# A hybrid decoder trunk on one core: the feed-forward input by Strassen's scheme on 6144 of 11264 columns, with the tokens stationary

## The chip, the core and the metric

One core of one Trainium2 chip runs the whole program in one launch. The metric is the device time of an execution in microseconds; of the kernel before three runs were timed. Engine names are those of the profile: PE is TensorE (PEld its weight loads), DVE VectorE, ACT ScalarE, POOL GpSimd, SP the engine that issues the DMAs.

## The reference

Two layers on 256 tokens of width 2048, all in float32. Layer 0 is a recurrent block (RG-LRU), layer 1 windowed attention with sinks; each is followed by the same feed-forward block, with hidden width 5632:

```
def swiglu_ffn(x, g, w_in, w_out):
    h = rms_norm(x, g)
    gate, up = jnp.split(h @ w_in, 2, axis=-1)
    return x + (jax.nn.silu(gate) * up) @ w_out
```

`w_in` is 2048 x 11264 (5632 gate and 5632 up columns). The change is about the product `h @ w_in`, which occurs twice.

## The kernel before, in words

**Weights as a stream of jobs.** All weights are cut into tiles of 128x1024 float32 (512 KB): two blocks of 128 input rows by four blocks of 128 columns. `stream` (line 272) goes through the list of jobs, one tile each. It issues a tile's DMA four jobs ahead (`LD`), into one of four buffers `raw`, and splits the tile three jobs ahead (`LC`): `split` (line 255) makes the rounded high part `hi` on ACT (line 260) and the rest `lo = raw - hi` on DVE (line 261). `hi` and `lo` have four buffers each.

**Matmuls.** Activations lie transposed (features on the partitions, 256 tokens along the row) and are split in the same way into 256 high and 256 low columns of one slot `s`. A job computes, for 2 x 4 blocks, `hi*xhi + hi*xlo + lo*xhi`: 24 matmuls with the weights stationary and 256 moving columns (line 324), or, where two belong together, one with 512. A group of eight jobs gives four blocks of 128 output columns in four PSUM banks. In the feed-forward input such a group holds two hidden tiles, gate and up of each; 22 groups give all 44.

**Beside the stream.** Other work is written as generators that `run_bg` (line 201) steps through, some at every half job, as long as a budget of DVE and ACT time per half job (`DVE_TICK`, `ACT_TICK`) lasts. `need` forces them on when a matmul wants a value that is not there yet. In `ffn` (line 513) the finished group is pulled out of PSUM, multiplied with the norm's factor `rstd`, put through Silu, multiplied and split for the output projection (`split_act`, line 411). The norm's factor is applied after the product, so that the product doesn't wait for the norm. The helpers `a`, `tt`, `stt`, `ts` record one ACT or DVE instruction each and carry their line (114, 123, 127, 132, 134) in the profile; `pe_other` (line 328) records PE's side work.

**POOL** runs only in the attention (lines 925, 927, 969). In `kv` (line 745) the shared key is spread over both partition halves by four matmuls with selection matrices `K_SEL0` and `K_SEL1` (line 796). The recording layer puts each engine's instructions into one list, which the engine goes through in order.

Of the kernel before, what the change touches and what calls it, by code (L numbers as in the profile page):

```python
# [17 lines left out]
P = 128  # L18
D = 2048
T = 256  # L20
# [15 lines left out]
K_ONE, K_BLK, K_SEL0, K_SEL1, K_ID = 0, 128, 256, 384, 512  # L36
K_HS, K_MASK = 640, 672
K_PREV, K_OWN = 672 + 384, 672 + 512
NCON = 672 + 640
# [10 lines left out]
class Trunk:  # L50
# [14 lines left out]
    RUNS = 3  # L65
    DVE_TICK = 640.0
# [188 lines left out]
    def split(self, i):  # L255
        raw, hi, lo = self.raw[i % 4], self.hi[i % 4], self.lo[i % 4]
# [15 lines left out]
    def stream(self):  # L272
        n = len(self.jobs)
        self.warm()
        for i in range(-self.LD, n):
            self.tick = 2 * i
            if i + self.LD < n:
                self.load(i + self.LD)
            if 0 <= i + self.LC < n:
                self.split(i + self.LC)  # L280
            if i >= 0:
                self.jobs[i][1](self.hi[i % 4], self.lo[i % 4])
            else:
                self.half_tick()
            self.run_bg()
        self.drain()

# [53 lines left out]
    def group(self, src, nk, xs, done, last=False, sync=(), paired=False, jobs=None, packed=False):  # L341
# [6 lines left out]
        for c in range(nk // 2):  # L348
            def mm(hi, lo, c=c):
                if c == 0:  # L350
# [13 lines left out]
                    st["begun"] = set()  # L364
                    self.hold = False
# [88 lines left out]
    def norm(self, r, wait=NORM):  # L454
# [8 lines left out]
        for b in range(2):  # L463
            self.pe_other(ps[:, T + b:T + b + 1], self.acc[:, b * P:(b + 1) * P],
                          self.con[:, K_ONE:K_ONE + 1], start=True, stop=True)
        yield 1
        y = self.rstd[r]
        m, t = self.nm, self.nt
        self.ts(m, ps[:, 0:T + 2], 1.0 / D, EPS, ALU.mult, ALU.add)
# [43 lines left out]
    def ffn(self, l, xs, r, gains, rn, out=None):  # L513
        hid = [Val() for _ in range(NH)]
        w = self.d[f"ffn_in{l}"]
        for g in range(NH // 2):
            def done(ps, g=g):
                rs = self.rstd[r][:, 0:T]
                early = not self.rv[r].ready
                v = [self.pull(p, r=None if early else rs) for p in ps]  # L520

                def task():
                    while not self.rv[r].ready:
                        yield 1
                    for h in range(2):
                        ga, up = v[2 * h], v[2 * h + 1]
# [5 lines left out]
                        self.tt(ga, ga, up, ALU.mult)  # L532
                        while not self.slots:
                            yield 1
                        s = self.slot()
# [209 lines left out]
    def kv(self, xs, r, gains):  # L745
# [7 lines left out]
        def done(ps):  # L753
# [5 lines left out]
            def task():  # L759
# [39 lines left out]
                for h in range(4):  # L799
                    self.split_act(self.kd[h].ap, ps[h // 2][:, h % 2 * T:h % 2 * T + T])  # L800
                    if h % 2:
                        self.free_mbank(ps[h // 2])
# [340 lines left out]
```

## Time and profile before

| | |
|---|---|
| median of 3 runs | 1984.31 us (1984.11 to 1984.93) |
| the profiled execution's own time | 1983.45 us |
| its span, first to last instruction | 1981.7 us |
| mean granted clock of TensorE | 1.0 |
| busy in the span: PE, DVE, ACT, POOL | 1975.0, 1257.6, 1063.0, 71.1 us |
| HBM read | 372.01 MB, 189 GB/s over the span |

The span lies inside the execution's time; 1.75 us are around it. A row of the profile's groups gives the line, the engine, the operation, what it writes and reads by the program's names, the shape, the count, then busy us and the mean in ns of one, then the idle time of the engine just before them and what ended it. A row of the timeline gives start, length, engine, line and operation; with x2 it stands for two in a row. Matmuls are pipelined, so a mean of PE is longer than the distance from one start to the next.

### The profile page before, as it was taken

How to read it: one execution, taken by the hardware profiler on the slowest of the kernel's cores; microseconds unless marked ns; L12 is line 12 of the kernel's file. 1: busy time of each engine (PE TensorE's matmuls, PEld its weight loads, DVE VectorE, ACT ScalarE, POOL GpSimd, SP SyncE). 2: the span in 40 equal slices, each digit the busy share in tenths (PEclk: the TensorE clock that was granted, in tenths of full speed). 3: DMA queues.
4: the chain of work that ended last, by engine and by line, in shares of the span. 5: the costliest groups of instructions: out<-in, count | busy, mean ns of one | idle time of the engine just before them, and what ended most of it. 6: DMA issues, size and time to landing. Idle time of an engine off the chain costs nothing.

```text
span 1981.7 us, 40161 instructions
## 1 busy us (share of the span) xinstructions
PE 1975.0 (100%) x16691; PEld 1932.8 (98%) x16691; DVE 1257.6 (63%) x1981; ACT 1063.0 (54%) x1608; POOL 71.1 (4%) x100
## 2 busy tenths in 40 slices
PE   9999999999999999999999999999999999999999
PEld 9999999999999999999999889999999999999999
DVE  8988876556556655545667776755665565554443
ACT  7798755444444444434556775644544454444342
POOL 0000000000000000000001451000000000000000
PEclk9999999999999999999999999999999999999999
DMA  8555655665566556566655345566666666666664
GB/s 283 189 183 182 213 192 192 195 197 192 192 193 195 195 194 192 193 194 197 193 184 168 129 128 163 189 194 197 194 192 194 193 190 199 193 193 205 206 207 127
DMA packets 105302, 376.71 MB, mean 190 GB/s; under 512 B 11808, under 2 KB 14240, under 8 KB 105120
## 3 DMA queue, kind: packets, MB, share of 16 engines
q1 hardware_dynamic: 104832, 374.01, 58.9%
q8 instruction: 130, 2.13, 0.4%
q14 instruction: 52, 0.43, 0.1%
q10 hardware_dynamic: 288, 0.14, 0.0%
HBM read 372.01 MB, written 2.10 MB: 189 GB/s over the span
## 4 chain that ended last, share of the span: by engine, by line
PE 96%; DVE 2%; ACT 2%; issue 0%; DMA 0%; POOL 0%; SPq 0%; ACTq 0%
PE b L324 92%; PE b L646 1%; ACT s L114 1%; PE b L335 1%; DVE s L905 1%; PE b L837 1%; ACT hi L260 0%; DVE lo L261 0%; PE b L332 0%; DMA raw<-in_lru_in 0%; DVE s L123 0%; PE b L847 0%; PE b L846 0%; PE b L848 0%; PE b L322 0%
## 5 line engine op out<-in xcount | busy, mean ns | idle before, releaser
L324 PE MATMUL b<-s,hi 128*128 128x256 f32 (+1 forms) x10317 | 1432.2, 284 | 1.2 <-ACT s L114 0.6
L324 PEld LDWEIGHTS b<-s,hi 128*128 128x128 f32 x10317 | 1316.1, 188 | 31.5 <-issue 1.4
L261 DVE TENSOR_TENSOR lo<-raw,hi 128x1024 fp32r<-128x1024 f32 (+1 forms) x705 | 861.7, 1223 | 654.0 <-ACT hi L260 652.1
L260 ACT ACTIVATE hi<-raw 128x1024 fp32r<-128x1024 f32 (+1 forms) x705 | 745.7, 1059 | 813.8 <-PE b L324 757.9
L324 PE MATMUL b<-s,lo 128*128 128x256 f32 x5504 | 827.8, 276 | 0.0
L324 PEld LDWEIGHTS b<-s,lo 128*128 128x128 f32 x5504 | 718.1, 188 | 0.5
L925 POOL TENSOR_TENSOR s<-s 128x128 f32<-128x128 f32 x32 | 14.6, 458 | 1109.6 <-ACT s L114 1100.9
L114 ACT ACTIVATE s<-h 128x256 fp32r<-128x256 f32 (+1 forms) x106 | 40.7, 411 | 23.9 <-DVE h L123 23.9
L114 ACT ACTIVATE t<-b 128x256 f32<-128x256 f32 x132 | 48.6, 374 | 2.2
L114 ACT ACTIVATE s<-x,par 128x256 fp32r<-128x256 f32 x80 | 38.5, 499 | 19.4 <-DVE x L123 13.7
L114 ACT ACTIVATE s<-s 128x256 f32<-128x256 f32 (+1 forms) x112 | 40.0, 412 | 5.7 <-DVE s L127 5.5
L114 ACT ACTIVATE h<-h 128x256 f32<-128x256 f32 (+1 forms) x104 | 38.9, 376 | 4.8 <-DVE h L123 2.7
L114 ACT ACT_TABLE_LOAD x30 | 38.5, 1283 | 0.5
L127 DVE SCALAR_TENSOR_TENSOR s<-x,par,s 128x256 fp32r<-128x256 f32 x80 | 37.2, 479 | 1.3 <-ACT s L114 0.7
L114 ACT ACTIVATE s<-s,h 128x128 f32<-128x128 f32 x64 | 28.3, 442 | 17.8 <-DVE h L132 10.8
L123 DVE TENSOR_TENSOR x<-x,b 128x256 f32<-128x256 f32 x64 | 24.1, 416 | 21.2 <-PE b L324 21.2
L123 DVE TENSOR_TENSOR h<-b,rstd 128x256 f32<-128x256 f32 x100 | 37.5, 414 | 0.0
L123 DVE TENSOR_TENSOR h<-h,rstd 128x256 f32<-128x256 f32 x94 | 35.3, 417 | 0.0
L123 DVE TENSOR_TENSOR h<-h,h 128x256 f32<-128x256 f32 x88 | 34.7, 416 | 0.4 <-ACT h L114 0.4
L123 DVE TENSOR_TENSOR s<-h,s 128x256 fp32r<-128x256 f32 x88 | 34.9, 417 | 0.1
L123 DVE TENSOR_TENSOR s<-s,s 128x256 fp32r<-128x256 f32 (+1 forms) x80 | 31.2, 419 | 5.7 <-ACT s L114 5.6
L123 DVE TENSOR_TENSOR h<-b,t 128x256 f32<-128x256 f32 x92 | 34.5, 415 | 0.0
(99 smaller groups left out, 625.4 us busy)
## 6 DMA issues: line engine op xcount, KB each, us to landing
raw<-in_ffn_in SPq DMA_DIRECT2D x352, 512.0 KB, 3.8
raw<-in_ffn_out SPq DMA_DIRECT2D x176, 512.0 KB, 4.2
raw<-in_lru_in SPq DMA_DIRECT2D x63, 512.0 KB, 4.0
raw<-in_lru_out SPq DMA_DIRECT2D x32, 512.0 KB, 4.3
raw<-in_w_q SPq DMA_DIRECT2D x32, 512.0 KB, 3.5
raw<-in_w_o SPq DMA_DIRECT2D x32, 512.0 KB, 3.5
raw<-in_gate SPq DMA_DIRECT2D x8, 512.0 KB, 4.3
raw<-in_kv SPq DMA_DIRECT2D x8, 512.0 KB, 4.4
```

Source lines behind the costliest of these rows:

```text
L114: self.nc.scalar.activation(out, in_, func, **kw)
L123: self.nc.vector.tensor_tensor(out, a, b, op)
L127: self.nc.vector.scalar_tensor_tensor(out, a, s, b, op0, op1)
L260: self.nc.scalar.activation(hi[:, q], raw[:, q], AF.Copy)
L261: self.nc.vector.tensor_tensor(lo[:, q], raw[:, q], hi[:, q].bitcast(F32), ALU.subtract)
L324: self.nc.tensor.matmul(*args, **kw)
L335: self.other = self.ins(f(*args, **kw))
L646: nc.tensor.matmul(out[j], (hi if high else lo)[:, c:c + P], x2[kt][:, q:q + T], start=kt == 0 and high > q, stop=kt == 1 and not high)
L837: nc.tensor.matmul(ps[f][:, 0:T], w0, x2[kt][:, q:q + T], start=k0 + kt == 0 and high > q, stop=k0 + kt == ND - 1 and not high)
L905: nc.vector.tensor_tensor_reduce(sc[hh][:, c0:c1], ps[hh][:, c0:c1], con[:, K_MASK + c0:K_MASK + c1], rr[:, b * 8 + f * 2 + hh:b * 8 + f * ...
L925: nc.gpsimd.tensor_tensor(o, o, sc[hh][:, 2 * P:3 * P], ALU.add)
```

## The change

The feed-forward input gets a plan of its own. Of 44 hidden tiles, six are computed as before (three head groups, kind W, while the norm is not known yet), then come six units, then one last group W. A unit is 16 steps in the order of `UNIT`: eight of kind S and eight of kind C.

- **S** takes four hidden tiles: 512 gate and 512 up columns. Tokens (2 x 128), input rows (2 x 1024) and columns (gate, up) are halved, and for each pair of row blocks p and p+8 the four weight blocks b11, b12, b21, b22 (128x512 each) and four token blocks give seven products in place of eight. The tokens are stationary, the 512 weight columns move; each product is three matmuls (high and low parts). Its two weight tiles are two jobs, of which the first carries two products and the second five. The seven weight operands are b11, b22, b21 and the differences t1 = b12 - b11, t2 = b22 - t1, t3 = b22 - b12, t4 = t2 - b21. DVE makes t1 and t2, POOL t3 and t4. Each of the seven is split: `hi` on ACT, `lo` on DVE for five and on POOL for two (b11 and t3).
- **C** is an ordinary weight tile: four row blocks by gate and up of one hidden tile, 24 matmuls of 256 columns into one bank.
- The seven products accumulate over the eight S steps of a unit in seven banks, C has the eighth. `four` adds them up at the unit's end (one ACT copy, seven DVE instructions of 512 columns), makes Silu and product, and eight PE transposes with ACT copies bring the result back to features on the partitions.
- `hi` and `lo` are now a ring of eight half tiles of 512 columns; a split goes ahead while the ring and three jobs allow.
- Normalised tokens (`nrm`) and their four sums and differences per pair (`mix`) are prepared and split once the norm is known; the sums are 4 x 8 POOL instructions of 128x128 a layer. Finished hidden tiles are kept unsplit and are split for the output projection behind the last unit (`activations`).
- Elsewhere: the key's spread in `kv` is four DMAs on ACT's queue (64 partitions x 512) in place of the four matmuls, the two narrow matmuls of a norm are left out where their result isn't used (three of four norms), and in the attention the mark that holds the side work back ends a job later.

Core of the diff:

```
+    UNITS, HEAD = 6, 3
+    UNIT = "SSCSCCSCSSCSCCSC"
+    SPARSE = (60.0, 120.0)
...
+        def ahead(i):
+            nonlocal split
+            while split < len(items):
+                j, at, size, f, _ = items[split]
+                if j > i + self.LC or at + size - 8 > freed:
+                    break
+                if f is None:
+                    self.split(j, at // 2 % 4)
+                else:
+                    f(j, *self.block(at))
+                split += 1
...
+            while done < len(items) and items[done][0] == i:
+                _, at, size, f, mm = items[done]
+                assert split > done
+                done += 1
+                if f is None:
+                    mm(self.hi[at // 2 % 4], self.lo[at // 2 % 4])
+                    freed = at + size
+                else:
+                    mm(*self.block(at))
+                    freed = at + size
+                    ahead(i)
+                    self.run_bg()
...
+                own = [slice(HD * (h % 2), HD * (h % 2) + HD) for h in range(4)]
                 for h in range(4):
-                    sel = (K_SEL0, K_SEL1)[h % 2]
-                    self.pe_other(ps[h // 2][:, h % 2 * T:h % 2 * T + T], con[:, sel:sel + P], sl[h // 2][:, 0:T],
-                                  start=True, stop=True)
+                    self.split_act(self.kd[h].ap[own[h], :], sl[h // 2][own[h], 0:T])
+                    yield
                 yield 1
                 for h in range(4):
-                    self.split_act(self.kd[h].ap, ps[h // 2][:, h % 2 * T:h % 2 * T + T])
-                    if h % 2:
-                        self.free_mbank(ps[h // 2])
+                    kd = self.kd[h].ap.bitcast(F32)
+                    nc.scalar.dma_start(kd[own[3 - h], :], kd[own[h], :])
                     self.kd[h].ready = True
                     yield
...
+        for u in range(cls.UNITS):
+            one, two = h, h + 1 + 4 * (u > 0)
+            h = two + 1
+            four = h + 1 if u + 1 < cls.UNITS else NH - 4
+            n = {"S": 0, "C": 0}
+            for kind in cls.UNIT:
+                c = n[kind]
+                n[kind] += 1
+                todo.append(("S", four, c, 0) if kind == "S" else ("C", (one, two)[c // 4], c % 4, c // 4))
+        while h + 4 < NH:
+            whole()
+        return todo
...
+        def activations():
+            for h in range(NH):
+                while not hid[h].ready or len(self.slots) < 2:
+                    yield 1
+                s = self.slot()
+                self.split_act(s, hid[h].ap)
...
+                act[h].ap = s
+                act[h].ready = True
+                yield
...
+        def prepare():
+            while not self.rv[r].ready:
+                yield 1
+            rs = self.rstd[r][:, 0:T]
+            for p in range(ND // 2):
+                v = []
+                for k in (p, p + ND // 2):
+                    t = self.half()
+                    self.stt(t, self.x[k // 4][:, k % 4, :], self.par[:, col + k:col + k + 1], rs, ALU.mult, ALU.mult)
+                    s = self.slot()
+                    self.split_act(s, t)
+                    nrm[k].ap = s
+                    nrm[k].ready = True
+                    v.append(t)
+                    yield
+                s = self.slot(F32)
+                s1, s2, s3, s4 = (s[:, i * P:i * P + P] for i in range(4))
+                a11, a21, a12, a22 = v[0][:, 0:P], v[0][:, P:T], v[1][:, 0:P], v[1][:, P:T]
+                for o, a, b, op in ((s1, a21, a22, ALU.add), (s2, s1, a11, ALU.subtract),
+                                    (s3, a11, a21, ALU.subtract), (s4, a12, s2, ALU.subtract)):
+                    nc.gpsimd.tensor_tensor(o, a, b, op)
+                for t in v:
...
+                self.a(hi, s)
+                self.tt(lo, s, hi.bitcast(F32), ALU.subtract)
...
+                mix[p].ap = (hi, lo)
+                mix[p].ready = True
+                yield
...
+        def pair(h, c, n):
+            def mm(hi, lo):
+                self.DVE_TICK, self.ACT_TICK = state["ticks"]
...
+                x = [self.need(nrm[4 * c + kt]) for kt in range(4)]
+                for part in range(2):
+                    for kt in (2 * part, 2 * part + 1):
+                        for f in range(2):
+                            q = slice(kt * 2 * P + f * P, kt * 2 * P + f * P + P)
+                            o = p[:, f * T:f * T + T]
+                            self.product(o, hi[:, q], x[kt][:, 0:T], kt + c + f == 0, False)
+                            self.product(o, hi[:, q], x[kt][:, T:2 * T], False, False)
+                    for kt in (2 * part, 2 * part + 1):
+                        for f in range(2):
+                            q = slice(kt * 2 * P + f * P, kt * 2 * P + f * P + P)
+                            self.product(p[:, f * T:f * T + T], lo[:, q], x[kt][:, 0:T], False, c == 3 and kt == 3)
...
+                if c == 3:
+                    ga = self.half()
+                    self.a(ga, p[:, 0:T], AF.Silu)
+                    self.tt(place(h), ga, p[:, T:2 * T], ALU.mult)
+                    hid[h].ready = True
...
+        def four(p, ps, h):
+            s1, s2, s3, s4 = (self.slot(F32) for _ in range(4))
+            self.a(s1, ps[1])
+            self.free_bank(ps[1])
+            self.tt(s2, ps[2], s1, ALU.add)
+            self.free_bank(ps[2])
+            yield
+            self.tt(s1, ps[6], s1, ALU.add)
...
+            self.free_bank(ps[4])
+            state["evict"] = None
+            yield
...
+            for ga, up in ((s2, s3), (s1, s4)):
+                self.a(ga, ga, AF.Silu)
+                yield
+                self.tt(ga, ga, up, ALU.mult)
+                self.free(up)
+                v.append(ga)
+                yield
+            one = self.con[:, K_ID:K_ID + P]
+            for j in range(2):
+                while not state["gap"] or not self.banks or not self.slots:
+                    yield 1
...
+                for q in range(2):
+                    for i in range(2):
+                        f = 2 * j + q
+                        self.pe_other(b[:, q * T + i * P:q * T + i * P + P], v[i][:, f * P:f * P + P], one,
+                                      f=nc.tensor.transpose)
+                yield 1
+                s = self.slot(F32)
...
+        def strassen(p, h):
+            last = p == ND // 2 - 1
+            def tiles(j):
+                a, b = self.raw[j % 4], self.raw[(j + 1) % 4]
+                return a[:, 0:512], a[:, 512:1024], b[:, 512:1024], b[:, 0:512]
+            def both(src, hi, lo, pool=False):
+                self.nc.scalar.activation(hi, src, AF.Copy)
+                (nc.gpsimd if pool else nc.vector).tensor_tensor(lo, src, hi.bitcast(F32), ALU.subtract)
+            def first(j, hi, lo):
+                if state["T"] is None:
+                    state["T"] = [self.slot(F32) for _ in range(4)]
+                b11, b12, b21, b22 = tiles(j)
+                t1, t2, t3, t4 = state["T"]
+                nc.vector.tensor_tensor(t1, b12, b11, ALU.subtract)
+                both(b11, hi, lo, True)
+            def second(j, hi, lo):
+                both(state["T"][0], hi, lo)
+            def third(j, hi, lo):
+                b11, b12, b21, b22 = tiles(j - 1)
+                t1, t2, t3, t4 = state["T"]
+                nc.gpsimd.tensor_tensor(t3, b22, b12, ALU.subtract)
+                nc.vector.tensor_tensor(t2, b22, t1, ALU.subtract)
+                nc.gpsimd.tensor_tensor(t4, t2, b21, ALU.subtract)
+                both(b22, hi, lo)
+            def raw(j, hi, lo):
+                both(tiles(j - 1)[2], hi, lo)
+            def diff(n):
+                def f(j, hi, lo):
+                    both(state["T"][n], hi, lo, n == 2)
+                    if n == 3 and last and h == NH - 4:
...
+            def mm(n):
+                def f(wh, wl):
+                    if n == 1:
+                        self.DVE_TICK, self.ACT_TICK = self.SPARSE
+                    if p == 0:
+                        state["banks"][n] = self.taken()
+                    o = state["banks"][n][:, :]
+                    k0, k1 = (self.need(nrm[k]) for k in (p, p + ND // 2))
+                    hi, lo = self.need(mix[p])
+                    i = {5: 0, 6: 1, 7: 2, 3: 3}.get(n)
+                    if i is not None:
+                        ah, al = (q[:, i * P:i * P + P] for q in (hi, lo))
+                    else:
+                        k, b = {1: (k0, 0), 2: (k1, 0), 4: (k1, 1)}[n]
+                        ah, al = (k[:, q * T + b * P:q * T + b * P + P] for q in range(2))
+                    self.product(o, ah, wh, p == 0, False)
+                    self.product(o, al, wh, False, False)
+                    self.product(o, ah, wl, False, last)
...
+            return ([(first, mm(1)), (second, mm(5))],
+                    [(third, mm(3)), (raw, mm(2)), (diff(1), mm(6)), (diff(2), mm(7)), (diff(3), mm(4))])
```

Three places in the lists of the engines. **DVE, in the middle of the feed-forward input, before**: the low parts of whole tiles (`lo<-raw,hi`) and, between two groups, the pull and the product of hidden tiles.

```order
L261 TENSOR_TENSOR lo_79<-raw_71,hi_75 128x1024
L123 TENSOR_TENSOR s_5239<-h_95,s_5239 128x256
L123 TENSOR_TENSOR s_5253<-h_97,s_5253 128x256
L261 TENSOR_TENSOR lo_80<-raw_72,hi_76 128x1024
L261 TENSOR_TENSOR lo_81<-raw_73,hi_77 128x1024
L261 TENSOR_TENSOR lo_82<-raw_74,hi_78 128x1024
```

**DVE at the same place now** (s_4312 is t1, s_4313 t2, s_4315 t4): one step S with the end of the S before it, and the C between.

```order
L789 TENSOR_TENSOR s_4312<-raw_72 128x512
L782 TENSOR_TENSOR lo_80<-s_4315,hi_76 128x512
L799 TENSOR_TENSOR s_4313<-raw_73,s_4312 128x512
L264 TENSOR_TENSOR lo_81<-raw_71,hi_77 128x1024
L782 TENSOR_TENSOR lo_82<-s_4312,hi_78 128x512
L782 TENSOR_TENSOR lo_79<-raw_73,hi_75 128x512 x2
L782 TENSOR_TENSOR lo_80<-s_4313,hi_76 128x512
L789 TENSOR_TENSOR s_4312<-raw_72 128x512
L782 TENSOR_TENSOR lo_81<-s_4315,hi_77 128x512
```

For an S, two weight tiles, seven instructions of 512 columns now stand in the place of two of 1024; a C has its one of 1024 as before; and t4's low part needs what POOL makes. **POOL, where it had nothing before** (s_4314 is t3): two steps S.

```order
L798 TENSOR_TENSOR s_4314<-raw_73,raw_72 128x512
L800 TENSOR_TENSOR s_4315<-s_4313,raw_73 128x512
L782 TENSOR_TENSOR lo_82<-raw_72,hi_78 128x512
L782 TENSOR_TENSOR lo_80<-s_4314,hi_76 128x512
L798 TENSOR_TENSOR s_4314<-raw_73,raw_72 128x512
L800 TENSOR_TENSOR s_4315<-s_4313,raw_73 128x512
L782 TENSOR_TENSOR lo_80<-raw_72,hi_76 128x512
L782 TENSOR_TENSOR lo_82<-s_4314,hi_78 128x512
```

Four instructions of 512 columns for each S, 384 in the program, each with both operands in SBUF.

240 lines of the change are left out of this document (198 added, 42 removed).

## The prediction

> **What bounds the kernel now.** First the page: its span, the busy time of the engines, the granted clock and the chain that ended last.
>
> ```profile
> span 1981.7 us, 40161 instructions
> PE 1975.0 (100%) x16691; PEld 1932.8 (98%) x16691; DVE 1257.6 (63%) x1981; ACT 1063.0 (54%) x1608; POOL 71.1 (4%) x100
> PEclk9999999999999999999999999999999999999999
> PE 96%; DVE 2%; ACT 2%; issue 0%; DMA 0%; POOL 0%; SPq 0%; ACTq 0%
> PE b L324 92%; PE b L646 1%; ACT s L114 1%; PE b L335 1%; DVE s L905 1%; PE b L837 1%; ACT hi L260 0%; DVE lo L261 0%; PE b L332 0%; DMA raw<-in_lru_in 0%; DVE s L123 0%; PE b L847 0%; PE b L846 0%; PE b L848 0%; PE b L322 0%
> ```
>
> TensorE is the bound at full clock: 92% of the chain is one line of matmuls. Second, a window that lies wholly in the feed-forward input, the stage that changes (columns: window, length, then busy us and instructions of PE, PEld, DVE, ACT, POOL, then clock, DMA share, GB/s).
>
> ```profile
> 394.00:586.00 192.00, 192.00 (x1614) 188.67 (x1613) 115.27 (x161) 92.92 (x125) 0.00 (x0) 1.00 0.61 193
> ```
>
> There PE never stops, DVE works 60% of the time, ACT 48%, and **POOL does nothing at all**. The price of the stage comes from a piece of the chain with 192 matmuls of 256 columns, the work of one weight group of eight jobs:
>
> ```profile
> 75.90 21.76 PE b L324 x192
> ```
>
> So 21.76 us a group, 2.72 us a job, 113.3 ns a matmul of 256. A unit of the new plan stands for six hidden tiles, which are three groups before: **65.3 us**. There are 12 units (6 in each layer). Everything below is the time of one unit against 65.3.
>
> **TensorE's side of the change.** A step S has 7 block products of 3 matmuls, each with 512 moving columns; a step C has the 24 matmuls of 256 that a job has now. A unit has eight of each, and eight transposes of 128x128 in fp32.
>
> ```profile
> L324 PE MATMUL b<-s,hi 128*128 128x256 f32 x9648 | 1302.2, 277 | 1.2 <-ACT s L114 0.6 <-ACT hi L260 0.6
> L324 PE MATMUL b<-s,hi 128*128 128x512 f32 x669 | 190.6, 392 | 0.0
> ```
> ```profile
> 1123.19 0.66 PE L335 MATMUL b<-con,s 128*128 128x128 f32 x4
> ```
>
> A matmul of 512 lasts 115 ns longer than one of 256, so its turn is 113 + 115 = 228 ns: no cheaper per column. S is 21 x 0.228 = 4.79 us, C is 2.72, and eight of both are 60.1 us. Four transposes take 0.66 us of which the last one's tail overlaps what follows; eight are about 1.0. PE needs 61.1 us a unit, **4.2 less than now**. If PE stayed the bound, 12 units would give back 50 us.
>
> **What DVE and POOL have to do for an S.** The scheme needs seven blocks of 512 weight columns where two jobs had four, each split into a high and a low part, and four of the seven are differences that must be made first. DVE gets 2 differences and 5 low parts, POOL 2 differences and 2 low parts, ACT 7 high parts. A C is split as a job is now. DVE's prices:
>
> ```profile
> L261 DVE TENSOR_TENSOR lo<-raw,hi 128x1024 fp32r<-128x1024 f32 x703 | 860.4, 1224 | 650.9 <-ACT hi L260 648.9
> L123 DVE TENSOR_TENSOR s<-s,s 128x256 fp32r<-128x256 f32 x48 | 18.8, 420 | 2.6 <-ACT s L114 2.5
> L261 DVE TENSOR_TENSOR lo<-raw,hi 128x512 fp32r<-128x512 f32 x2 | 1.4, 692 | 3.2 <-ACT hi L260 3.2
> ```
> ```profile
> 641.89 0.75 DVE L123 TENSOR_TENSOR h<-b,t 128x256 f32<-128x256 f32 x2
> ```
>
> 512 columns cost 0.69 us alone. Two of 256 in a row cover 0.75, not 0.84, so one that follows directly costs 0.09 less: 0.60 for 512, and 1.14 for a C's 1024. Alone, DVE would need 7 x 0.60 + 1.14 = 5.3 us for an S and a C. ACT, by the same reading:
>
> ```profile
> L260 ACT ACTIVATE hi<-raw 128x1024 fp32r<-128x1024 f32 x703 | 744.4, 1060 | 813.0 <-PE b L324 757.9 <-issue 36.2 <-PE b L848 5.9
> L260 ACT ACTIVATE hi<-raw 128x512 fp32r<-128x512 f32 x2 | 1.3, 630 | 0.8 <-DMA raw<-in_lru_in 0.8
> ```
>
> 7 x 0.63 + 1.06 = 5.5 us. POOL has no instruction of 512 elements in this trace. The nearest rows, in which DVE ran nothing that hindered them (128 elements; 256 with a whole tile as second operand; two of 256 with a broadcast column as second operand):
>
> ```profile
> 1120.33 0.46 POOL L925 TENSOR_TENSOR s<-s 128x128 f32<-128x128 f32 x1 [1.39 <-ACT s L114]
> ```
> ```profile
> 1103.19 0.75 POOL L969 TENSOR_TENSOR s<-s,con 128x256 f32<-128x256 f32 x1 [2.50 <-ACT s L114]
> ```
> ```profile
> 1122.00 1.18 POOL L927 TENSOR_TENSOR s<-s,h 128x256 f32<-128x256 f32 x2 [0.34 <-DVE s L123]
> ```
>
> From 128 to 256 elements the second form adds 0.29 us, the third 0.13. Carried on, 512 elements are 0.75 + 2 x 0.29 = **1.33 us** or 0.59 + 2 x 0.13 = **0.85 us**. The new instructions read two whole tiles, as the first two rows do, so I take 1.33 and keep 0.85 as the low end. Four of them are 5.3 us for each S and C. Each of the three engines alone is thus under PE's 7.5 us for the pair.
>
> **They are not alone.** In the attention stage POOL and DVE meet, and the rows show what happens.
>
> ```profile
> 1131.78 2.17 POOL L927 TENSOR_TENSOR s<-s,h 128x256 f32<-128x256 f32 x2
> ```
> ```profile
> 1132.21 1.27 DVE L261 TENSOR_TENSOR lo<-raw,hi 128x1024 fp32r<-128x1024 f32 x1 [0.46 <-ACT hi L260]
> ...
> 1133.54 1.49 DVE L261 TENSOR_TENSOR lo<-raw,hi 128x1024 fp32r<-128x1024 f32 x1
> ```
>
> The same two POOL instructions that took 1.18 us above take 2.17 when a low part of 1024 columns begins between them: 0.99 more, nearly all of DVE's 1.22. The DVE instruction at 1133.54 begins while POOL is still busy (to 1133.95) and takes 1.49 in place of 1.22. A second pair of rows:
>
> ```profile
> 1084.83 2.58 POOL L969 TENSOR_TENSOR s<-s,con 128x256 f32<-128x256 f32 x2
> ```
> ```profile
> 1085.60 1.21 DVE L261 TENSOR_TENSOR lo<-raw,hi 128x1024 fp32r<-128x1024 f32 x1
> ```
>
> Undisturbed these two POOL instructions would be about 1.57 (0.75 and a start 0.82 later). So a DVE instruction with two SBUF operands and a POOL instruction do not run side by side; one stands until the other has finished. Only a start-up passes under the other's hold: POOL ends at 1133.95, 0.47 after DVE's end at 1133.48, in place of 0.59 (0.12 hidden), and DVE ends at 1135.03, 1.08 after POOL, in place of 1.22 (0.14 hidden). The Trainium skill, SBUF — State Buffer, section "Who interferes with whom", says that a Vector instruction with two SBUF inputs contends with a GpSimd instruction that reads SBUF, and that the one that comes first has the shared ports for its whole instruction. The trace agrees (0.99 and 0.27 us of waiting in the rows above), though by these rows the wait is some 0.1 us short of the whole instruction.
>
> All 11 instructions of an S are of this kind, and DVE's low part of a C too. So their times add up. POOL behind DVE: 1.33 - 0.12 = 1.21. DVE behind POOL: 0.69 - 0.14 = 0.55; behind itself 0.60. An S: 4 x 1.21 + 4 x 0.55 + 3 x 0.60 = **8.84 us**. With a C's 1.14: 9.98 for the pair, where PE needs 7.51 and now has 8.16 for the same columns. Eight pairs: 79.8 us. At a unit's end DVE also empties seven banks, 7 instructions of 512 with one operand in PSUM (0.60 each, 4.2 us); they don't hold POOL up, which can do two of its own beside them (2.4), so 1.8 are left, and two products in SBUF add 1.2. **A unit is 82.8 us, 17.5 more than now; 12 units are +210 us.** PE waits a quarter of the unit; the lead of eight half tiles of split weights is some 5 us and is used up once.
>
> The Trainium skill, GPSIMD Engine Reference, section "3.1 Elementwise", has the only price for long operands: about 2.6 cycles per element at 1.2 GHz for two inputs, which I estimate at 1.11 us for 512; with it in the place of 1.21 the sum would be 2154 us. No run here shows that instruction.
>
> **The other edits.** Normalised tokens and their sums (per layer 16 gains, 16 splits, 8 mixed splits, 20 us of DVE by the rows above) fall into the three head groups, where DVE is idle 40% of 65.3 us: nothing. The 44 splits of the hidden tiles move behind the last unit; 44 x 0.42 = 18.5 us of DVE beside 1.22 in each 2.72 us job fit in the first dozen jobs, and the output projection uses them in that order: nothing, and 20 us a layer if they came before it. The head selection in K loses four fp32 matmuls and gains four small DMAs eight jobs ahead of their use, and three norms lose two small matmuls each: together -2 us. Eviction and transposes lie in PE's waits. DMA needs three tiles of 512 KB in 10 us, 157 GB/s, under today's 193.
>
> **The sum.** The profiled execution took 1983.45 us, 0.9 below the median. 1983.45 + 210 - 2 = 2191, and with the 0.9: **2192 us**.
>
> **Rivals.**
> 1. *Faster: PE stays the bound.* POOL's work is hidden beside DVE's. Then -50 - 2: **1932 us**. For it: each engine alone fits (5.3, 5.5, 5.3 against 7.5). Against it: the waiting in the rows. It decides where an S and C pair takes (65.3 - 3.0) / 8 = 7.79 us, that is at 0.66 us for a POOL instruction behind DVE, half of the 1.21, and under the low end of 0.73.
> 2. *They exclude each other, but POOL is quick on plain tiles* (0.85, behind DVE 0.73). S is 6.92, the pair 8.06, the unit 67.5: +26 - 2, **2008 us**. The row for it has a broadcast operand, which the new instructions lack.
> 3. *Nothing of a start-up is hidden, and the order on each engine leaves both idle at times* (a POOL difference needs one of DVE's, whose low part needs POOL's). S is 4 x 1.33 + 7 x 0.69 = 10.2, the pair 11.4, the unit with 9 x 0.69 at its end 97: +380, **2364 us**.
>
> **How the numbers follow.** The forecast gets 0.66: the exclusion stands in rows in both directions, the count of instructions is certain, and POOL's price is the open size. Rival 1 has 0.15, rival 2 0.10, rival 3 0.08, and 0.01 is left for no change. The range from 2000 to 2310 takes in the forecast with its sizes, rival 2 and the nearer half of rival 3, some 0.80. Faster by over 0.2% (about what a measurement of this kernel can tell from no change) has 0.15, within it 0.01, slower 0.84.
>
> **What the new profile would show.** Right: 384 POOL instructions of 128x512 whose mean is well over 1.33 us because the wait is in it; DVE's 512 low parts over 0.69; in the feed-forward input PE busy about three quarters with idle time released by POOL and DVE, DVE and POOL together near the whole window, GB/s down to about 155. Wrong: POOL at 0.7 us or less, or DVE and POOL busy times in that window whose sum is far over its length while PE stays full; then the two run side by side and rival 1 holds.

## The result, and the profile after

The changed kernel takes **2276.59 us** (median of 4 runs, 2274.16 to 2277.54), the kernel before 1984.21 (1983.70 to 1984.93): a ratio of 1.1473, with a 95% interval of 1.1459 to 1.1486. It is slower, as forecast, by 292 us where 208 were forecast, and inside the range given.

The page of the new profile, in the lines that answer to those of before:

```profile
span 2275.8 us, 38297 instructions
PE 2064.2 (91%) x14484; PEld 1865.6 (82%) x14484; DVE 1824.5 (80%) x2377; ACT 1246.6 (55%) x2080; POOL 781.8 (34%) x548
...
PEclk9999999999899999999999999989999999999999
```

TensorE has fallen from 100% to 91%, DVE has risen by 567 us and POOL by 711, though POOL was given only 384 + 64 short instructions. No engine is full over the whole program, so the share alone names no bound. The table by stretches of 70 us does (columns: window, length, then busy us and instructions of PE, PEld, DVE, ACT, POOL, then clock, DMA share, GB/s); the first row is the head groups, the second lies inside the units, the third is two whole units:

```profile
292.00:357.00 65.00, 63.55 (x511) 61.50 (x509) 56.75 (x89) 36.71 (x60) 20.25 (x28) 1.00 0.53 167
...
495.00:565.00 70.00, 57.53 (x278) 46.01 (x276) 64.24 (x61) 36.41 (x61) 46.08 (x27) 0.93 0.41 141
```
```profile
538.20:710.70 172.50, 144.44 (x740) 118.12 (x739) 160.42 (x150) 87.69 (x142) 111.06 (x64) 0.92 0.43 147
```

In the two units DVE is busy 93% of the time and POOL 64%. Added up these are 271 us in a window of 172.5, which looks like two engines side by side. The groups by shape show that it isn't (count, then busy us and mean ns):

```profile
L800 POOL TENSOR_TENSOR s<-s,raw 128x512 f32<-128x512 f32 x96 | 175.4, 1827 | 90.3 <-DVE s L799 54.1 <-DVE lo L782 20.2 <-ACT hi L781 8.7
...
L798 POOL TENSOR_TENSOR s<-raw,raw 128x512 f32<-128x512 f32 x96 | 159.2, 1658 | 151.4 <-DMA raw<-in_ffn_in 130.6 <-PE b L898 15.8 <-issue 3.1
```
```profile
L782 DVE TENSOR_TENSOR lo<-s,hi 128x512 fp32r<-128x512 f32 x288 | 297.9, 1045 | 0.6 <-ACT hi L781 0.3
L782 DVE TENSOR_TENSOR lo<-raw,hi 128x512 fp32r<-128x512 f32 x192 | 262.2, 1382 | 0.0
...
L126 DVE TENSOR_TENSOR s<-b,s 128x512 f32<-128x512 f32 x72 | 48.2, 676 | 0.0
```

The same low part of 512 columns that took 692 ns before now has a mean of 1045 or 1382; the sums with one operand in PSUM (last row) take 676. The extra time is waiting that a row counts as busy. Single instructions in the timeline (start, length) show who waits for whom:

```profile
657.43 1.31 POOL L798 TENSOR_TENSOR s<-raw,raw 128x512 f32<-128x512 f32 x1 [0.38 <-DMA raw<-in_ffn_in]
657.51 1.77 DVE L782 TENSOR_TENSOR lo<-s,hi 128x512 fp32r<-128x512 f32 x1
...
660.95 0.68 DVE L782 TENSOR_TENSOR lo<-s,hi 128x512 fp32r<-128x512 f32 x1
...
661.17 1.62 POOL L800 TENSOR_TENSOR s<-s,raw 128x512 f32<-128x512 f32 x1 [2.43 <-DVE s L799]
661.55 1.78 DVE L782 TENSOR_TENSOR lo<-raw,hi 128x512 fp32r<-128x512 f32 x1
```

POOL's first instruction takes 1.31 us; the DVE instruction that begins 0.08 later ends at 659.28, 0.54 after POOL's end. The next POOL instruction begins beside a DVE instruction that ends at 661.63, and ends itself at 662.79, 1.16 later. That is one instruction at a time, with a little of the start-up hidden. It holds over the whole trace: DVE's instruction of 512 columns ends 0.55 us after POOL's in 295 such meetings (0.54 to 0.56), POOL's 1.15 us after DVE's in 319 (1.12 to 1.26). Only ten of the 384 POOL instructions have no DVE instruction beside them; they take 1.27 to 1.31 us.

Counted from the records, DVE or POOL has an instruction running for 164.2 of the 172.5 us; for the other 8.3, 4.2 a unit, both stand. Raw weight tiles are waited for now (the whole program: us in total, times, longest):

```profile
POOL s L798 <- DMA raw<-in_ffn_in: 130.6, 43, 5.6
...
ACT hi L781 <- DMA raw<-in_ffn_in: 104.0, 42, 5.2
```

POOL's difference t3 and ACT's high parts wait for raw weight tiles, which the kernel before never let happen in this stage. These waits alone don't say what both engines stand for, since DVE can run meanwhile. The gaps in which neither runs do: in the eight units that are neither first nor last of a layer they are 35 us, and 33 of them end when a raw tile has landed for which DVE's t1 or t2 waits.

A unit is measured at TensorE, from the first matmul of a layer's first S to the first matmul of the group W behind the last unit, over six. In layer 0 that is from 366.5 to 894.1 us, in layer 1 from 1479.8 to 2009.0: 87.9 and 88.2 us, against 65.3 for the same columns before and 82.8 forecast. Twelve units are +273 of the 292.

### The profile page after: what moved, and what is told of

It reads as the page before. It is cut to its first block, busy times and chain, and to the rows that moved or that the text cites. A ratio compares the mean times of both kernels' runs of the same rounds, so it can differ in the third digit from the quotient of the medians.

```text
span 2275.8 us, 38297 instructions
## 1 busy us (share of the span) xinstructions
PE 2064.2 (91%) x14484; PEld 1865.6 (82%) x14484; DVE 1824.5 (80%) x2377; ACT 1246.6 (55%) x2080; POOL 781.8 (34%) x548
## 5 line engine op out<-in xcount | busy, mean ns | idle before, releaser
L365 PE MATMUL b<-s,hi 128*128 128x256 f32 (+1 forms) x6016 | 835.9, 285 | 10.5 <-ACT hi L263 7.6
L365 PEld LDWEIGHTS b<-s,hi 128*128 128x128 f32 x6016 | 766.5, 188 | 29.7 <-ACT hi L263 8.8
L365 PE MATMUL b<-s,lo 128*128 128x256 f32 x3200 | 477.7, 278 | 4.2 <-DVE lo L264 3.9
L898 PE MATMUL b<-hi,s 128*128 128x512 f32 x1324 | 438.9, 410 | 40.0 <-DVE s L126 35.3
L781 ACT ACTIVATE hi<-s 128x512 fp32r<-128x512 f32 x384 | 236.3, 626 | 233.8 <-PE b L898 79.1
L898 PEld LDWEIGHTS b<-hi,s 128*128 128x128 f32 x1324 | 249.5, 196 | 107.8 <-ACT hi L781 22.9
L898 PE MATMUL b<-lo,s 128*128 128x512 f32 x672 | 282.2, 424 | 50.9 <-DVE lo L782 48.8
L782 DVE TENSOR_TENSOR lo<-s,hi 128x512 fp32r<-128x512 f32 x288 | 297.9, 1045 | 0.6 <-ACT hi L781 0.3
L782 DVE TENSOR_TENSOR lo<-raw,hi 128x512 fp32r<-128x512 f32 x192 | 262.2, 1382 | 0.0
L898 PE MATMUL b<-s,hi 128*128 128x256 f32 x1536 | 235.6, 300 | 13.7 <-ACT hi L263 13.6
L898 PEld LDWEIGHTS b<-s,hi 128*128 128x128 f32 x1536 | 219.7, 208 | 26.5 <-ACT hi L263 18.9
L798 POOL TENSOR_TENSOR s<-raw,raw 128x512 f32<-128x512 f32 x96 | 159.2, 1658 | 151.4 <-DMA raw<-in_ffn_in 130.6
L800 POOL TENSOR_TENSOR s<-s,raw 128x512 f32<-128x512 f32 x96 | 175.4, 1827 | 90.3 <-DVE s L799 54.1
L898 PE MATMUL b<-s,lo 128*128 128x256 f32 x768 | 138.5, 306 | 55.9 <-DVE lo L264 55.4
L782 POOL TENSOR_TENSOR lo<-s,hi 128x512 fp32r<-128x512 f32 x96 | 158.4, 1650 | 66.7 <-ACT hi L781 61.1
```

Source lines behind the costliest of these rows:

```text
L365: self.nc.tensor.matmul(*args, **kw)
L781: self.nc.scalar.activation(hi, src, AF.Copy)
L782: (nc.gpsimd if pool else nc.vector).tensor_tensor(lo, src, hi.bitcast(F32), ALU.subtract)
L798: nc.gpsimd.tensor_tensor(t3, b22, b12, ALU.subtract)
L800: nc.gpsimd.tensor_tensor(t4, t2, b21, ALU.subtract)
L898: self.nc.tensor.matmul(o, w, x, start=start, stop=stop, skip_group_check=True)
```

## The experiments

The theory behind the prediction is that a DVE instruction with two SBUF operands and a POOL instruction that reads SBUF exclude each other, so that a unit costs the sum of both. Its rivals are that POOL is merely slow, that DVE alone is overloaded, that the loss is outside the units, and that the raw tiles come late. Each experiment below is an edit of the changed kernel unless it says otherwise.

**All of an S on DVE.** POOL's four instructions are given to DVE, which gets more work and no company:

```
-                (nc.gpsimd if pool else nc.vector).tensor_tensor(lo, src, hi.bitcast(F32), ALU.subtract)
+                nc.vector.tensor_tensor(lo, src, hi.bitcast(F32), ALU.subtract)
-                nc.gpsimd.tensor_tensor(t3, b22, b12, ALU.subtract)
+                nc.vector.tensor_tensor(t3, b22, b12, ALU.subtract)
-                nc.gpsimd.tensor_tensor(t4, t2, b21, ALU.subtract)
+                nc.vector.tensor_tensor(t4, t2, b21, ALU.subtract)
```

> POOL's four instructions of an S go to DVE, which then has 11 of 512 columns; POOL has nothing in the stage. Theory A (a DVE instruction with two SBUF operands and a POOL instruction exclude each other, so their times add): an S is 11 x 0.60 = 6.6 us of DVE in the place of 8.84 of both, the pair with a C 7.74, the unit 61.9 + 5.4 for the banks and products = 67 to 71 us in the place of 87; 2010 to 2070 us in all. Theory B (DVE's own load is the limit, and POOL takes some off it): 8 x 4 x 0.60 = 19 us more in each unit, about 2500 us. Theory C (the chain t1, t2, t4, split, matmul is the limit, whatever engine makes them): little change, 2230 to 2280 us.

Measured: 2042.59 us, ratio 1.0287 (1.0270 to 1.0305). Its low parts, and two of its units:

```profile
L782 DVE TENSOR_TENSOR lo<-s,hi 128x512 fp32r<-128x512 f32 x384 | 252.2, 687 | 5.0 <-ACT hi L781 4.3
L782 DVE TENSOR_TENSOR lo<-raw,hi 128x512 fp32r<-128x512 f32 x288 | 197.6, 687 | 0.3
```
```profile
567.10:704.70 137.60, 131.42 (x740) 108.80 (x739) 136.88 (x216) 88.57 (x144) 0.00 (x0) 1.00 0.57 184
```

The time is in the range of theory A. One engine does the work of two in 68.8 us a unit instead of 87: 234 us are won by taking a helper away. Each instruction is back at 687 ns, and DVE is now the bound, busy 136.88 of 137.60 us. POOL's help was worth less than nothing.

**POOL writes, but doesn't read.** Each of POOL's four instructions becomes three fills of 512 columns with zeros, so that POOL is still occupied (the real t3 and t4 and two low parts are left out):

```
-                nc.gpsimd.tensor_tensor(t3, b22, b12, ALU.subtract)
+                for _ in range(3):
+                    nc.gpsimd.memset(t3, 0.0)
```

> Each of POOL's four instructions of an S is replaced by three fills with zeros of the same 512 columns, so that POOL is busy but reads nothing; t3, t4 and the low parts of b11 and t3 are zero in this kernel, that part of the computation is left out. Theory A: if it is the reads that meet, DVE no longer waits, its 512 low parts fall to 0.69 us, PE is the bound at 61 us a unit: 1935 to 1965 us. If any POOL instruction holds DVE up, DVE's instructions stay lengthened and the time stays over 2100 us. Theory B (DVE's own load): DVE is as loaded as in the changed kernel, so 2230 to 2280 us. Theory C (the chain through POOL): the fills need nothing from DVE, which cuts the chain too, so it expects what A does; e1 tells these two apart.

Measured: 1984.35 us, ratio 0.9997 (0.9986 to 1.0007).

```profile
L784 POOL MEMSET lo<- 128x512 f32 x576 | 301.8, 527 | 129.2 <-PE b L904 123.7
```
```profile
L786 DVE TENSOR_TENSOR lo<-s,hi 128x512 fp32r<-128x512 f32 x288 | 196.5, 687 | 11.8 <-ACT hi L781 10.0
```
```profile
450.00:640.00 190.00, 189.19 (x1107) 164.08 (x1107) 151.94 (x226) 134.08 (x214) 139.63 (x288) 1.00 0.58 200
```

POOL is busy 73% of the window and DVE 80%, side by side, with DVE's instructions at 687 ns. So it is POOL instructions that read SBUF (here two operands each) that shut DVE out, not POOL's being busy. The Trainium skill, SBUF — State Buffer, section "Who interferes with whom", says that an instruction of DVE with two SBUF inputs contends with a GpSimd instruction that reads SBUF and not with one that only writes it. The trace agrees: 687 ns beside fills, 1045 and 1382 beside reads. The size was missed, though: with POOL's price gone and TensorE full (189.19 of 190.00) the kernel only equals the one before, where 1935 to 1965 had been expected. A unit takes 63.9 us in layer 0 and 63.2 in layer 1, not 61.1; why is told below.

**Three units instead of six in each layer** (`UNITS, HEAD = 3, 3`; the groups that are freed go through the ordinary plan).

> Three units in each layer in the place of six; the columns left go to ordinary groups. If the loss is in the steady part of each unit (88.3 us against 65.3 in the two traces, 12 units, and 16 us once), the time is 1984 + 16 + 6 x 23 = 2138 us. If the loss lay mostly in starting and ending the plan of a layer, it would stay over 2200 us.

Measured: 2152.63 us, ratio 1.0845 (1.0824 to 1.0867), 15 us over the 2138 expected and far from the 2200 of the other theory. Half of the units leave 168 of 292 us, so the loss goes with the units. They take 90.3 and 89.6 us here: the first of a layer, which is the longest, has more weight, and that makes about 10 of the 15.

**Five raw buffers instead of four**, with the DMAs five jobs ahead (and one slot fewer, for space):

```
-    LD = 4
+    LD = 5
-        self.raw = [const.tile([P, 1024], F32, name=f"raw{i}") for i in range(4)]
+        self.raw = [const.tile([P, 1024], F32, name=f"raw{i}") for i in range(5)]
```

> Five buffers for raw weight tiles and DMAs five jobs ahead, in the place of four (and one slot fewer, for space). In the changed kernel's steady units DVE and POOL are both idle for some 4 us a unit, with waits put down to the DMA of a tile. If a buffer that an S gives back late is the cause, a fifth takes most of it away: unit 83 to 85 us, 2215 to 2250 us. If the waits only stand in for others, nothing changes: 2265 to 2280 us.

Measured: 2256.74 us, ratio 1.1370 (1.1353 to 1.1387): 20 us less, between the two expectations. POOL's wait for raw tiles falls from 130.6 to 81.1 us, the later units of a layer from between 86 and 88 us to between 84 and 86. So buffers are a part of the loss, and a fifth does not take all of that part away.

**POOL keeps only t3 and t4**; all seven low parts are DVE's.

> POOL keeps the two differences t3 and t4 of a step S, all seven low parts go to DVE. Theory A (a DVE and a POOL instruction with SBUF operands exclude each other, so their times add): S is 2 x 1.21 + 2 x 0.55 + 7 x 0.60 = 7.72 us, the pair with a C 8.86, a unit 71 + 3 at its end + about 2 of idle = 74 to 77, between the 68.6 of the run with all on DVE and the 87 of the change: 2105 to 2150 us in all. Theory B (what costs is that POOL is slow or waits for tiles, not the exclusion): the two low parts on POOL were its least urgent work and nothing is gained by moving them, 2250 to 2285 us.

Measured: 2187.97 us, ratio 1.1026 (1.1004 to 1.1048), outside of both expectations. The direction is the first theory's, 89 us won by moving two of four instructions; the size is not. Two units:

```profile
601.60:765.20 163.60, 139.26 (x736) 112.05 (x735) 148.84 (x182) 88.13 (x142) 54.75 (x32) 0.96 0.49 154
```

By the records, DVE or POOL runs for 152.6 of these 163.6 us: 76.3 a unit, against a sum of 73.9, and both stand for 5.5. I had put 2 us for standing. Of the gaps in which neither runs, 6.1 us in the two units end with a raw tile for DVE's t1 or t2 and 3.4 us with a high part from ACT; what makes those late with only two instructions on POOL was not tried.

**Three units and six raw buffers.** (With six units, six buffers don't fit beside the other tiles. Here three slots fewer make room, and the DMAs go six jobs ahead.)

> Three units in each layer as in the run with three, and six buffers for raw tiles with their DMAs six jobs ahead, in place of four. If the time in which DVE and POOL both stand (5 to 6 us a unit) is waiting for raw tiles: units of 84 to 85 in place of 90, 2115 to 2125 us. If it is the order in which the engines wait for each other: units of 88 to 90, 2140 to 2155 us.

Measured: 2133.09 us, ratio 1.0747 (1.0726 to 1.0769), 20 less than with four buffers and between the two expectations. Waits for raw tiles, and a window with about a unit's instructions:

```profile
ACT hi L781 <- DMA raw<-in_ffn_in: 39.5, 8, 6.4
...
POOL s L798 <- DMA raw<-in_ffn_in: 23.7, 7, 6.6
```
```profile
440.00:523.00 83.00, 71.34 (x363) 59.08 (x362) 78.09 (x76) 43.88 (x72) 55.37 (x32) 0.90 0.46 152
```

With four buffers the same two waits were 48.7 and 78.5 us. In this window DVE or POOL runs for 81.8 of 83.0 us. From DVE's first difference to that of the next unit, the second unit of layer 0 and the first two of layer 1 take 84.1, 81.8 and 84.1 us, of which both engines stand for 1.2, 2.2 and 0.8: with the tiles there, a unit comes down to about the sum of the two engines, which the prediction had at 82.8. Over all six units the gain is 3 to 4 us each, not the 5 to 6 expected: the first unit of layer 0 still takes 94.6.

**Three units and a ring of ten half tiles** of split weights instead of eight.

> Three units in each layer, four raw buffers, and a ring of ten half tiles of split weights in place of eight. If the time in which DVE and POOL both stand comes from a full ring (ACT's high part waits until TensorE has used a half tile, and DVE and POOL wait for ACT): units of 85 to 87 in place of 90, 2120 to 2135 us. If not: 2148 to 2156 us.

Measured: 2157.83 us, ratio 1.0872 (1.0850 to 1.0894), 5 us more than without, with intervals that overlap, where 18 to 33 us less were expected if the ring were too short. The ring is not what both engines stand for.

**The tokens' sums on DVE**, POOL's four instructions of an S left as they are:

```
-                    nc.gpsimd.tensor_tensor(o, a, b, op)
+                    nc.vector.tensor_tensor(o, a, b, op)
```

> The change with only the 128-column sums of the tokens (4 x 8 a layer) moved from POOL to DVE; the steps S keep their four instructions on POOL. If POOL and DVE meeting in the head groups is what makes the first step S late (6 us in layer 0, 12 in layer 1, against the run with four units): 2258 to 2268 us, units as in the change, 86 to 88. If the head was late by DVE's work as such: 2272 to 2285 us.

Measured: 2260.61 us, ratio 1.1381 (1.1362 to 1.1400), 16 us less and inside the first range. The first matmul of an S starts at 359.79 us instead of 366.51 in layer 0; in layer 1, counted from the first matmul of `kv`, after 309.6 us instead of 321.6. In the changed kernel those sums stood thus:

```profile
L642 POOL TENSOR_TENSOR s<-h,h 128x128 f32<-128x128 f32 x16 | 14.7, 917 | 17.6 <-DVE h L130 17.6
```

917 ns for 128 columns, which took 460 alone in the profile before: the same meeting of POOL and DVE, in the head groups. On DVE the same sums take 352 ns.

**Four units of eight S and sixteen C, nothing on POOL**, the sums included. A unit stands for four groups, and DVE has more time for each S.

```
-    UNITS, HEAD = 6, 3
-    UNIT = "SSCSCCSCSSCSCCSC"
+    UNITS, HEAD = 4, 3
+    UNIT = "SCCSCCSSCCSCCSCCSCCCSCCC"
```

> Everything on DVE, the 128-column sums of the tokens too, and four units in place of six, each with 16 steps C (four hidden tiles) to its eight S: 4096 of 11264 columns by the scheme. A unit stands for four groups, 87.0 us of the kernel before. By PE it needs 8 x 4.79 + 16 x 2.72 + 1.0 = 82.8 us, by DVE 8 x 7.2 (11 x 0.65) less what stands side by side + 16 x 1.14 + 5 = about 80. If PE is then the bound and the stall at a unit's end is the 3 us seen in the run with POOL writing only: 8 x (82.8 + 3 - 87.0) = -10, with the head 0 to +13 late: 1972 to 1988 us. If the stall at the end goes because DVE has more room: 1950 to 1965 us. If DVE stays the bound as in the run with all on DVE: 2000 to 2040 us.

Measured: 2006.54 us, ratio 1.0111 (1.0095 to 1.0126). The time lies in the third range, which was meant for DVE as the bound, but TensorE is nearer to full (97% of the window, DVE 91%), so that hit is luck:

```profile
440.00:710.00 270.00, 262.07 (x1692) 235.57 (x1691) 244.89 (x377) 167.11 (x270) 0.00 (x0) 0.99 0.60 189
```

A unit takes 89.7 and 91.0 us where 82.8 were worked out for TensorE. Part of it is a stop at each unit's end, where DVE empties the banks (three of these stops, of up to 2.7 us, in 270 us). Another part is the distance of the matmuls; the starts of an S and of the two C steps behind it, in which TensorE does not stop:

```profile
412.14 0.63 PE L898 MATMUL b<-hi,s 128*128 128x512 f32 x2
...
417.04 1.10 PE L898 MATMUL b<-s,hi 128*128 128x256 f32 x8
...
422.69 0.63 PE L898 MATMUL b<-hi,s 128*128 128x512 f32 x2
```

21 matmuls of 512 columns in 4.90 us are 233 ns each, 48 of 256 in 5.65 us are 118. The prediction had 228 and 113.3, from the kernel before. With the new steps TensorE needs 8 x 4.90 + 16 x 2.82 + 1.0 = 85.3 us a unit, and of the 4.2 that the scheme was to save in 87.0 there are 1.7 left, less than the 2.6 to 3.1 us a unit for which TensorE stands in the units. Another 1 to 3 us of a unit are not accounted for; in layer 1 part of them is the clock, which is at half for 13.7 us of its four units.

**The same with four head groups** ahead of the first unit.

> As the run with four units, with four groups W ahead of the first unit in place of three (and one less behind the last). If the tokens' splits and sums are late for the first step S (the lateness of about 6 us a layer seen in the change), 6 to 12 us are won back against the run with four units; if the first step S is not late there, within 2 us of it.

Measured: 2009.58 us, ratio 1.0131 (1.0114 to 1.0148). One group more ahead doesn't help; the 3 us more are within the two intervals. The first S starts at 382.4 us, 22.1 after the 360.3 of the run above, about one group (21.8), and in both runs TensorE never stops in the 100 us ahead of it: with the sums on DVE it was not late.

**The kernel before with only the edits outside the feed-forward input.**

> The kernel before with only the edits outside the feed-forward input: the key's spread by four DMAs, the narrow matmuls of three norms left out, the later mark in the attention. By the working of the prediction -2 us: 1981 to 1984 us. If the DMAs come late for the scores, up to 5 us slower: 1985 to 1990 us.

Measured: 1982.53 us, ratio 0.9991 (0.9981 to 1.0000): 1.5 us less, in keeping with the 2 us that the prediction gave them, though the interval reaches no change.

**The kernel before with RUNS = 0.** An attempt at the slower step of the matmuls.

> The kernel before with one constant changed, RUNS = 0: the groups of three matmuls of 512 columns that it puts in behind a side job of TensorE are left out, their columns done by matmuls of 256. In the units of the change matmuls of 256 start 118 ns apart and those of 512 start 233 apart, in the kernel before 113 and 228 to 229. Theory A (TensorE keeps a slower step of 5 ns more after a side job or a wait, until such a group of three ends it): most of the 16000 matmuls then go at 118, +40 to +80 us: 2025 to 2065 us. Theory B (the slower step belongs to the stationary tokens or to the order of the scheme's products): the step stays 113, 1980 to 1995 us.

Measured: 1985.72 us, ratio 1.0006 (0.9996 to 1.0017). It tells less than it should: the number of 512-column matmuls only falls from 680 to 581, since the job's own plan asks for the others. Starts 117 to 119 ns behind a matmul of 256 rise from 1140 to 1402 in the records, 262 times 5 ns or 1.3 us; a difference of that size can't be told from none here. Theory A, by which most matmuls would go at the slower step, is out; what sets the step stays open.

## Why the prediction was right, and where its sizes were off

**The mechanism held.** A DVE instruction with two SBUF operands and a POOL instruction that reads SBUF don't run side by side; moving POOL's share to DVE wins 234 us, and putting fills that read nothing in its place (with that part of the work left out) wins 292. A POOL that is merely slow would gain by both runs too; what speaks against it is that DVE's own instructions are stretched by POOL's reads (1045 and 1382 ns) and not by its fills (687 ns), and the 0.55 and 1.15 us of the meetings. The prices that had to be carried over from shorter rows held. POOL's 512 columns: 1.27 to 1.31 us where 1.33 was taken and 0.85 kept as the low end; the 1.11 estimated beside them was too low. POOL behind DVE: 1.15 for 1.21. DVE behind POOL: 0.55 for 0.55. The sum of a unit: 82.1 us with DVE or POOL running, in place of 82.8. Still, +292 us is 1.4 times the +208 forecast, 33 us inside the range, and the two large misses below go the same way.

**The unit: 88.1 us for 82.8, +63 us in all. The largest miss.** The prediction took the sum of the two engines as the unit's time, which holds only if one of them always has something to do. In the later units of a layer both stand for 3.9 to 5.4 us; a layer's first unit is longer still, 96.8 and 90.8 us from DVE's first difference to that of the next unit, against 86.0 to 87.6 later. Both engines stand for 8.8 and 7.1 us there, and in layer 0 DVE has 84 instructions in it in place of 75, so that one of the two runs for 87.9 us. The prediction named standing in its third rival, as two engines that wait for each other, at 97 us a unit. What the runs show is something else: raw tiles that come late. They end nearly all gaps of the later units. With six buffers three of the four units that can be measured in this way take 81.8 to 84.1 us, with 0.8 to 2.2 us of standing; a longer ring does nothing. A raw buffer can be filled again when its last reader has finished. Of the kernel's DMA issues 54 wait for a low part on POOL (280.1 us in all) and 22 for POOL's t3 (62.0 us), which were no readers of a raw buffer before. So, as I read it, the readers stand in line behind each other on two engines, and the next tile, 3.6 us on its way, is asked for that much later. The prediction looked at DMA's rate alone (157 GB/s, under today's 193) and not at when a buffer comes free.

**The tokens and their sums: "nothing" was wrong, 16 us.** The prediction counted DVE's idle time in the head groups and forgot its own finding there: the sums are POOL instructions that read SBUF, beside DVE's low parts. The run with the sums on DVE gives the 16 us back. With the 63 that makes 79 of the 84 us by which the forecast was short.

**TensorE's side: 61.1 us a unit was too good.** It was no term of the forecast, but it was all of rival 1. At 233 and 118 ns a unit needs 168 x 0.233 + 192 x 0.118 + 1.0 = 62.8 us, and the run in which POOL only writes takes 63.9 and 63.2. Against 65.3 that is 21 us in twelve units, and the late head, whose sums are still on POOL in that run, takes most of it back. So the rival's 1932 us was not to be had even with the exclusion gone, and "-50 us if TensorE stayed the bound" was mis-sized.

**What the profile was to show.** 384 POOL instructions of 512 columns with a mean of 1.65 to 1.83 us: right. DVE's low parts over 0.69: right. GB/s of 131 to 148 where "about 155" stood: the unit is longer. TensorE busy 82% of the window where "three quarters" stood; its need is 62.8 of 88, or 71%, and most of the rest goes with a lowered clock (below). DVE and POOL together near the whole window: right, 164.2 of 172.5 us. The sign against the forecast, busy times whose sum is far over the window, was badly chosen: the sum is 271 us although the two do not run side by side, because a row counts waiting as busy. Only its other half, a full TensorE, tells the cases apart. The side edits, -2: their own run gave -1.5. The 2364 us of rival 3 leave these 2 us out; its sum is 2362.

No version tried beats the kernel before by more than can be told. By this accounting the scheme has 2.5 us a unit to gain on TensorE at best, 30 us in all, and the run with all on DVE shows that its DVE work alone fills 68.4 us of a unit that had 65.3.

## What to carry to other kernels

Before work is shared between DVE and POOL, add up their instructions that read two SBUF tiles nearly as if one engine did them all (here 0.55 and 1.15 us behind each other, 0.69 and 1.29 alone); if the sum is over the bound's time, the split loses, and in the runs here it lost to DVE alone. Then ask when each buffer comes free under the slower pace, since the transfers start from there and not from the mean bandwidth. And price a new matmul pattern by its own distance of starts: 5 ns a matmul took 1.7 of the 4.2 us that a unit was to gain here.

## What the runs showed of the hardware that was not expected

**TensorE's clock can halve after a short stop.** In the changed kernel TensorE stops for 2.4 us, waiting for a low part, and then goes at half the clock (the timeline, then the window behind it; the clock is the column ahead of the last two):

```profile
878.89 1.22 PE L898 MATMUL b<-s,lo 128*128 128x256 f32 x4 [2.37 <-DVE lo L264]
```
```profile
879.00:882.00 3.00, 3.00 (x14) 3.00 (x15) 3.00 (x2) 1.22 (x4) 2.65 (x2) 0.50 0.49 175
```

The matmuls of 256 columns start 213 ns apart there, and the trace has the clock at half from 878.6 to 882.0 us, 3.4 us. Not every such stop is followed by it: from 300 us on, a stretch at half clock begins in the stop or within 3.5 us behind it for 9 of the 15 stops of 2.0 to 2.5 us and for all 8 over 3 us. The Trainium skill, TensorE: Matmul & The Clock Gate, section "Part 1: The HAM clock gate (the "warmup" mystery)", gives half the clock after an idle window of some 3.4 us and full clock after as long a busy one. The trace agrees on the half and on the length of the slow stretch; the stop ahead of it was shorter. The windows' 0.90 to 0.95 are means of such stretches. Where TensorE waits for DVE and POOL anyway, this should cost little; that was not tried.

**A slower step of TensorE.** 118 and 233 ns from start to start in the units against 113 and 228 in most of the kernel before; it was tried once, and not explained.

**Fills on POOL cost 527 ns for 512 columns and don't slow DVE** (687 ns for its low parts), nor do POOL's reads slow DVE's sums of 512 columns with an operand in PSUM: 40 of the 84 run beside a POOL instruction, and those take 676 ns as the others do.
